# Two transformer blocks in float32 on one core: the low parts of 202 weight blocks made by an accumulating DMA

## The chip, the cores and the metric

The kernel runs on one core of a Trainium2 chip, as one program. Its metric is the device time of one execution in microseconds (us); the median of several executions counts.

## What is computed

Two stacks of two layers each, on 512 tokens of width 1024, all in float32. The first stack has a latent attention mixer (MLA) and a differential attention mixer, the second a convolution and pooling mixer ("even") and a mixer of forgetting attention and a long convolution ("odd"). Behind each mixer stand a residual and a layer norm, then a gated feed-forward layer, again with residual and norm:

```python
for i in range(DEPTH):
    mix = _mla_mixer(h, ...) if i % 2 == 0 else _diff_mixer(h, ...)
    h = _layernorm(ALPHA * h + mix, ln_mix_g[i], ln_mix_b[i])
    h = _layernorm(ALPHA * h + _swiglu(h, ffn_w_gu[i], ffn_w_down[i]), ln_ffn_g[i], ln_ffn_b[i])
for layer in range(DEPTH):
    mix = even_mixer(x, ...) if layer % 2 == 0 else odd_mixer(x, ...)
    x = layer_norm(ALPHA_2 * x + mix, ln_mix_g[layer], ln_mix_b[layer])
    x = layer_norm(ALPHA_2 * x + swiglu(x, ffn_w_in[layer], ffn_w_out[layer]), ...)

def _swiglu(x, w_gu, w_down):
    gate, up = jnp.split(x @ w_gu, 2, axis=-1)
    return (jax.nn.silu(gate) * up) @ w_down
```

Nearly all the work is matrix products with weights that are read once.

## The kernel before

**Split products.** TensorE works on a rounded type (F32R in the code). Each float32 operand is therefore kept as a high part, which is the operand rounded to F32R, and a low part, the operand minus the high part. `mm3` makes each product from three matmuls: high by high (L370), one high by low (L371) and the other (L372). Everything that a product reads needs its low part by the second or third matmul.

**Weights.** `weight_plan` lists 300 weight blocks of 128 partitions by up to 1024 columns (512 KB) in the order in which the stages use them. `Weights.load` (L162) fetches a block from HBM with a DMA on SyncE's queue (SP) into a tile `wraw`; there are two such tiles, taken in turn. `Weights.split` makes the high part `whi` on ScalarE (ACT, L169) and the low part `wlo` on VectorE (DVE) or, for a few, on GpSimd (POOL) (both L170); `whi` and `wlo` have five tiles each. So a `wraw` tile is free, and the load of the block after the next can start, when a block's low part has been made; and a `whi` tile is free when TensorE has used the block that stood in it. `Weights.ahead(n)`, called by hand in the order of the program, splits a few blocks ahead of use; `LOOK` is 2.

**Two forms of product.** 76 of the 300 entries ("win": most of the gate and up columns of the four feed-forward layers) are multiplied in a seven-product form, whose blocks are combined on VectorE first and come in four splits per entry through a `wraw` ring of their own. The other 224 are single splits: the mixers' projections (`mla_a`, `mla_b`, `uq_r`, `uq_n`, `ukv`, `df_q`, `df_k`, `df_v`, `ev_in`, `od_a`, `od_g`, `od_x`, `od_v`, `od_q`, `od_k`), their output projections (`mla_o`, `df_o`, `ev_o`, `od_o`), the first `gate` and `up` blocks of a feed-forward layer and all its `down` blocks.

**Stages.** MLA (to 201 us of the profiled span), feed-forward (to 554), differential attention (to 806), feed-forward (to 1158), even (to 1300), feed-forward (to 1651), odd (to 1891), feed-forward (to the end). One block is 24 matmuls of 512 columns, or as much work in other shapes.

**The seams.** A stage ends in `project_out`: the last products, then a layer norm per 128 tokens (sums on VectorE, squares on ScalarE, the root on GpSimd, gains and biases on VectorE), transposes on TensorE, high and low parts of the result. The first four products of the next stage are issued there too (`first`): over the first 256 tokens for blocks one to four, in between the last token tile's transposes, then over the other 256. In `project_out` the order on TensorE, VectorE and ScalarE is the order in which the code is written (`by_hand`); `W.ahead(2)`, `(3)`, `(4)` and `(5)` stand among it. Elsewhere a scheduler sets each engine's order. GpSimd also issues the DMAs of the norms' gains and biases (`lng`, `lnb`, L418) there, on a queue of its own.

Of the kernel before, what the change touches and what calls it, by code (L numbers as in the profile page):

```python
# [9 lines left out]
F32 = mybir.dt.float32  # L10
F32R = mybir.dt.float32r
BF16 = mybir.dt.bfloat16
AF = mybir.ActivationFunctionType
OP = mybir.AluOpType
# [38 lines left out]

ONPOOL = ("uq_n", "ukv", "df_o", "mla_o")
OTHERWISE = (11, 12, 15, 20, 23, 24, 25, 73, 79, 80, 81, 82, 83, 84, 85, 86, 88, 90, 91, 100, 102, 103)
NORM_ACT = (1, 3, 6, 7, 12, 13, 16, 24, 25, 26, 30)
ROPE_POOL = (1, 2, 3, 4, 5, 7, 9, 11)
DUP_ACT = (0, 2, 4, 6)
# [83 lines left out]
class Weights:  # L142
# [23 lines left out]
    def split(self, pool, raw, o, n, eng):  # L166
        tiles = [p.tile([P, UNIT], F32R, name="w" + k, tag="w" + k) for p, k in zip(pool, ("hi", "lo"))]
        hi, lo = [x[:, :n] for x in tiles]
        self.nc.scalar.activation(hi, raw[:, o:o + n], AF.Copy)  # L169
        eng.tensor_sub(lo, raw[:, o:o + n], hi.bitcast(F32))  # L170
        return tiles

    def steps(self):

        while self.loaded < min(len(self.plan), self.at + 2) and (
                self.loaded == self.at or self.plan[self.loaded][0] != "win" or self.sums is not None):
            self.load()
        name, raw, n = self.got[self.at]
        self.at += 1
        nc = self.nc  # L180
        if name != "win":
            on_pool = (name in ONPOOL) != (self.at - 1 in OTHERWISE)
            self.ready.append((name, *self.split((self.hi, self.lo), raw[0], 0, n, nc.gpsimd if on_pool else nc.vector)))
            return

        gate, up = raw
        H = UNIT // 2
        a11, a12, a21, a22 = gate[:, :H], gate[:, H:], up[:, :H], up[:, H:]
        pg = self.split((self.hi, self.lo), gate, 0, UNIT, nc.vector)
        yield  # L190
        pu = self.split((self.hi, self.lo), up, H, H, nc.vector)
        nc.vector.tensor_add(a22, a21, a22)
        nc.vector.tensor_sub(a21, a11, a21)
        yield
        su = self.split(self.sums, up, 0, UNIT, nc.vector)
        nc.vector.tensor_sub(a11, a22, a11)
        nc.vector.tensor_sub(a12, a12, a11)
        yield
        sg = self.split(self.sums, gate, 0, UNIT, nc.vector)

        def part(tiles, o):
            return [x[:, o:o + H].rearrange("p (k n) -> p k n", n=P) for x in tiles]

        self.ready.append((name, {
            1: part(pg, 0), 2: part(pg, H), 3: part(sg, H), 4: part(pu, 0), 5: part(su, H), 6: part(sg, 0), 7: part(su, 0)}, None))
# [107 lines left out]
def kernel(ctx: ExitStack, tc: tile.TileContext, a: dict, out: bass.AP):  # L313
# [393 lines left out]
    def ffn(xpool_cm, xT, key, i, ps, names):  # L707
# [3 lines left out]
        with pool("ffn") as fp:  # L711
# [3 lines left out]
            def hidden(j, g, u):  # L715
                nc.vector.tensor_mul(g, g, u)
                h = fp.tile([P, S], F32R, name="hh", tag="hh", bufs=HID)
                l = fp.tile([P, S], F32R, name="hl", tag="hl", bufs=HID)
                split(h, l, g)
                chunks[j] = (h, l)  # L720
# [112 lines left out]
    def mla(xT, close_x, open_x, names):  # L833
        with pool("mla_o") as op_:
            cmask = op_.tile([P, S], F32, name="cmask")
            with ExitStack() as st:
# [28 lines left out]
                def turn_c(j, h, l):  # L865
                    ps = pst()
                    for t in range(NT):
                        nc.tensor.transpose(ps[:, t * P:(t + 1) * P], cq[:, t, j * P:(j + 1) * P], ident)
                    split(h, l, ps, par("g_q", j) if j < 3 else par("g_kv", j - 3))
# [67 lines left out]
                def head(h):  # L937
                    p, i = divmod(h, 2)
                    if i == 0:
                        WP[p] = W.next("uq_n", 3, 256), W.next("ukv", 2, 512)  # L940
                    wq, wk = WP[p]
                    m = slice(i * P, (i + 1) * P)
                    got = []
                    for s, (w, k, x, sc) in enumerate((
                            (wq, 3, (cqh, cql), -MLA_SCALE),
                            (wk, 2, (ckh, ckl), None))):
                        ps = acc()
                        project_T(ps, w, x, k, m=m)
                        hi = ap_.tile([P, S], F32R, name="qh", tag=f"qh{s}", bufs=2)
                        lo = ap_.tile([P, S], F32R, name="ql", tag=f"ql{s}", bufs=2)  # L950
                        split(hi, lo, ps, sc)
                        got += [hi, lo]
                    Q[h] = got
# [39 lines left out]
                def rest(h, pt, qb, n, e, sums):  # L993
                    nc.vector.reciprocal(sums[:, 2:3], sums[:, 1:2])
                    if 4 * h + qb in NORM_ACT:
                        nc.scalar.activation(e[:, :n], e[:, :n], AF.Copy, scale=sums[:, 2:3])
# [905 lines left out]
```

## Time and profile before

| | us |
|---|---|
| three runs | 2255.45, 2256.09 (median), 2257.32 |
| the profiled execution | 2255.44 |
| its span, first to last instruction | 2253.7 |
| TensorE busy in the span | 2194.6 |
| VectorE busy | 1753.4 |
| ScalarE busy | 998.2 |
| GpSimd busy | 132.1 |

The mean granted TensorE clock over the span is 0.993. A busy TensorE counts pipelined matmuls whose ends overlap, so 97% is no statement on its peak; the idle rest, 59 us, is what all waits of TensorE together cost.

### The profile page before, as it was taken

To read this page: it belongs to the slowest core of one execution; us is meant where nothing else is said; L and a number is where in the kernel's file an instruction comes from. 1 tells how busy PE (TensorE), PEld (TensorE's weight loads), DVE (VectorE), ACT (ScalarE), POOL (GpSimd) and SP (SyncE) were. 2 spreads that over 40 slices of the span, in tenths; PEclk is the share of its full clock that TensorE was granted. 3 is DMA by queue.
4 is the path that set the end of the run, shared out by engine and by line. 5 is a ranking of instruction groups with operands and counts; after the bars stand their busy time and mean duration, and the time that the engine had idled before them with its cause. 6 is when DMAs were issued, how large, how long until landed. Compare 5 with 4: busy or idle time off the path is not lost. (4 is left out here: it accounts for less than half of the span.)

```text
span 2253.7 us, 35104 instructions
## 1 busy us (share of the span) xinstructions
PE 2194.6 (97%) x14076; PEld 1971.3 (87%) x14076; DVE 1753.4 (78%) x2871; ACT 998.2 (44%) x1669; POOL 132.1 (6%) x138
## 2 busy tenths in 40 slices
PE   8999999999999999999999999999999889999997
PEld 8888999998988789999988899999988767999996
DVE  5767988887666688888765588888679987988886
ACT  4654444333665554443333244433336655444331
POOL 2200000001321100000010000000010000000001
PEclk9999999999999999999999999999999899999999
DMA  5213332332321133333323233333232102233331
GB/s 174 64 48 103 94 113 94 113 94 75 111 79 63 47 108 107 104 94 113 94 98 95 75 131 107 104 100 108 90 99 93 57 19 103 94 113 94 113 94 56
DMA packets 59363, 210.48 MB, mean 93 GB/s; under 512 B 6624, under 2 KB 6880, under 8 KB 59200
## 3 DMA queue, kind: packets, MB, share of 16 engines
q1 hardware_dynamic: 56304, 198.97, 27.8%
q0 software_dynamic: 2320, 8.23, 1.1%
q8 instruction: 110, 1.80, 0.3%
q10 hardware_dynamic: 576, 1.05, 0.1%
q14 instruction: 53, 0.43, 0.1%
HBM read 206.12 MB, written 2.10 MB: 92 GB/s over the span
## 5 line engine op out<-in xcount | busy, mean ns | idle before, releaser
L169 ACT ACTIVATE whi<-wraw 128x1024 fp32r<-128x1024 f32 (+2 forms) x528 | 520.4, 988 | 838.8 <-PE acc L371 501.7
L170 DVE TENSOR_TENSOR wlo<-wraw,whi 128x1024 fp32r<-128x1024 f32 (+2 forms) x502 | 568.2, 1133 | 126.2 <-ACT whi L169 123.3
L371 PE MATMUL acc<-xl,whi 128*128 128x256 f32 (+1 forms) x1712 | 522.9, 305 | 3.5 <-DVE xl L480 3.5
L372 PE MATMUL acc<-xh,wlo 128*128 128x256 f32 (+1 forms) x1712 | 522.2, 305 | 2.6 <-DVE wlo L170 2.5
L370 PE MATMUL acc<-xh,whi 128*128 128x256 f32 (+1 forms) x1712 | 523.6, 306 | 0.4 <-DVE kl L1097 0.4
L371 PEld LDWEIGHTS acc<-xl,whi 128*128 128x128 f32 x1712 | 322.5, 188 | 29.2 <-DVE xl L480 4.7
L370 PEld LDWEIGHTS acc<-xh,whi 128*128 128x128 f32 x1712 | 322.4, 188 | 25.6 <-DVE kl L1097 0.5
L372 PE MATMUL acc<-xs,wlo 128*128 128x256 f32 x1216 | 341.3, 282 | 0.0
L371 PE MATMUL acc<-xql,whi 128*128 128x256 f32 x1216 | 341.0, 281 | 0.0
L372 PEld LDWEIGHTS acc<-xh,wlo 128*128 128x128 f32 x1712 | 322.6, 188 | 18.9 <-DVE wlo L170 3.8
L370 PE MATMUL acc<-xs,whi 128*128 128x256 f32 x1216 | 339.0, 280 | 0.0
L371 PEld LDWEIGHTS acc<-xql,whi 128*128 128x128 f32 x1216 | 228.5, 188 | 5.5
L370 PEld LDWEIGHTS acc<-xs,whi 128*128 128x128 f32 x1216 | 229.6, 189 | 3.5
L372 PEld LDWEIGHTS acc<-xs,wlo 128*128 128x128 f32 x1216 | 228.1, 188 | 0.3
L370 PE MATMUL tr<-whi,hh 128*128 128x512 f32 (+1 forms) x296 | 117.8, 398 | 0.0
L781 DVE TENSOR_TENSOR sums<-sums,acc 128x512 f32<-128x512 f32 x76 | 52.3, 688 | 83.9 <-PE acc L372 83.3
L371 PE MATMUL tr<-wlo,hh 128*128 128x512 f32 (+1 forms) x296 | 116.8, 395 | 0.0
L372 PE MATMUL tr<-whi,hl 128*128 128x512 f32 (+1 forms) x296 | 115.8, 391 | 0.0
L372 PE MATMUL ps<-whi,hl 128*128 128x512 f32 x288 | 113.7, 395 | 0.0
L370 PE MATMUL ps<-whi,hh 128*128 128x512 f32 x288 | 113.4, 394 | 0.0
L371 PE MATMUL ps<-wlo,hh 128*128 128x512 f32 x288 | 113.2, 393 | 0.0
L430 DVE SCALAR_TENSOR_TENSOR res<-res,acc 128x512 f32<-128x512 f32 x87 | 59.1, 683 | 58.1 <-PE acc L372 57.7
(364 smaller groups left out, 3959.5 us busy)
## 6 DMA issues: line engine op xcount, KB each, us to landing
wraw<-in_gu_dram SPq DMA_DIRECT2D x176, 512.0 KB, 3.5
wraw<-in_dn_dram SPq DMA_DIRECT2D x88, 512.0 KB, 3.4
wraw<-in_ev_in_dram SPq DMA_DIRECT2D x16, 512.0 KB, 3.5
wraw<-in_mla_o_dram SPq DMA_DIRECT2D x8, 512.0 KB, 3.5
wraw<-in_df_q_dram SPq DMA_DIRECT2D x8, 512.0 KB, 3.5
wraw<-in_df_k_dram SPq DMA_DIRECT2D x8, 512.0 KB, 3.5
wraw<-in_df_v_dram SPq DMA_DIRECT2D x8, 512.0 KB, 3.5
wraw<-in_df_o_dram SPq DMA_DIRECT2D x8, 512.0 KB, 3.4
```

Of the source, the lines that this page charges most:

```text
L169: self.nc.scalar.activation(hi, raw[:, o:o + n], AF.Copy)
L170: eng.tensor_sub(lo, raw[:, o:o + n], hi.bitcast(F32))
L370: nc.tensor.matmul(ps, ah, bh, start=first, stop=False)
L371: nc.tensor.matmul(ps, ah, bl, start=False, stop=False)
L372: nc.tensor.matmul(ps, al, bh, start=False, stop=last)
L430: nc.vector.scalar_tensor_tensor(y, y, ALPHA if first else 1.0, ps, op0=OP.mult, op1=OP.add, accum_out=SUMS[t][:, c:c + 1] if sums else None)
L781: nc.vector.tensor_add(g[:, 1:3], g[:, 1:3], v)
```

## The change

For blocks named in a new tuple, the low part no longer comes from one subtraction on VectorE or GpSimd. ScalarE writes the negated high part, rounded to F32R, into `wlo` (a second pass over `wraw`, with scale -1), and a DMA that GpSimd issues adds `wraw` to it in SBUF. The result is again the block minus its high part.

```diff
+BYDMA = ("od_x", "od_v", "od_q", "od_k", "od_o", "down", "df_q", "df_k", "df_v", "df_o", "ev_in", "ev_o", "mla_o", "gate", "up")
@@ split
         self.nc.scalar.activation(hi, raw[:, o:o + n], AF.Copy)
-        eng.tensor_sub(lo, raw[:, o:o + n], hi.bitcast(F32))
+        if eng is None:
+            self.nc.scalar.activation(lo, raw[:, o:o + n], AF.Copy, scale=-1.0)
+            self.nc.gpsimd.dma_start(lo.bitcast(F32), raw[:, o:o + n], accum_op=OP.add)
+        else:
+            eng.tensor_sub(lo, raw[:, o:o + n], hi.bitcast(F32))
@@ steps
-            self.ready.append((name, *self.split((self.hi, self.lo), raw[0], 0, n, nc.gpsimd if on_pool else nc.vector)))
+            self.ready.append((name, *self.split((self.hi, self.lo), raw[0], 0, n, None if name in BYDMA else nc.gpsimd if on_pool else nc.vector)))
```

By the plan 202 of the 300 blocks are named so: 181 were subtracted on VectorE and 21 on GpSimd. The 304 splits of the seven-product form and 22 blocks (`mla_a`, `mla_b`, `uq_r`, `uq_n`, `ukv`, `od_a`, `od_g`) stay as they were. Lines move by five: the high part is L170 in the new kernel, the negation L172, the DMA L173, the old subtraction L175.

The first place is ScalarE at the seam between the MLA mixer and its feed-forward layer, from the second block's high part on; `whi_2267`, `whi_2289` and `whi_2302` are the second, third and fourth block of the feed-forward layer (the old `up`, `gate`, `up`). Before:

```order
L169 ACTIVATE whi_2267<-wraw_2076 128x1024
L448 ACTIVATE junk_2281,lns_2243<-res3_81,lns_2243 128x1024
L169 ACTIVATE whi_2289<-wraw_2265 128x1024
L476 ACTIVATE xh_2055<-tr_2271 128x4x128
L476 ACTIVATE xh_2055<-tr_2276 128x4x128
L469 COPY xq_2060<-tr_2271 128x4x128
L169 ACTIVATE whi_2302<-wraw_2287 128x1024
```

And now, the same blocks with the numbers 2276, 2299 and 2313:

```order
L170 ACTIVATE whi_2276<-wraw_2084 128x1024
L172 ACTIVATE wlo_2277<-wraw_2084 128x1024
L453 ACTIVATE junk_2291,lns_2252<-res3_81,lns_2252 128x1024
L170 ACTIVATE whi_2299<-wraw_2274 128x1024
L172 ACTIVATE wlo_2300<-wraw_2274 128x1024
L481 ACTIVATE xh_2061<-tr_2281 128x4x128
L481 ACTIVATE xh_2061<-tr_2286 128x4x128
L474 COPY xq_2066<-tr_2281 128x4x128
L170 ACTIVATE whi_2313<-wraw_2297 128x1024
L172 ACTIVATE wlo_2314<-wraw_2297 128x1024
```

Each negation stands right behind its high part, and nothing else has moved.

The second place is GpSimd's queue at the same seam: `lnr` are the norms' roots, `lng` and `lnb` the loads of gains and biases. Before:

```order
L388 TENSOR_TENSOR lnr_2140<-lnv_2138,mhalf_93 128x1
L388 TENSOR_TENSOR lnr_2159<-lnv_2157,mhalf_93 128x1
L388 TENSOR_TENSOR lnr_2224<-lnv_2222,mhalf_93 128x1
L418 DMA lng_2548<-in_ln_ffn_g_dram 128x1024
L388 TENSOR_TENSOR lnr_2285<-lnv_2283,mhalf_93 128x1
L418 DMA lnb_2549<-in_ln_ffn_b_dram 128x1024
```

And now:

```order
L393 TENSOR_TENSOR lnr_2149<-lnv_2147,mhalf_93 128x1
L393 TENSOR_TENSOR lnr_2168<-lnv_2166,mhalf_93 128x1
L393 TENSOR_TENSOR lnr_2233<-lnv_2231,mhalf_93 128x1
L173 DMA wlo_2277<-wraw_2084 128x1024
L423 DMA lng_2562<-in_ln_ffn_g_dram 128x1024
L393 TENSOR_TENSOR lnr_2295<-lnv_2293,mhalf_93 128x1
L173 DMA wlo_2300<-wraw_2274 128x1024
L423 DMA lnb_2563<-in_ln_ffn_b_dram 128x1024
L173 DMA wlo_2314<-wraw_2297 128x1024
```

The DMAs of the second, third and fourth block stand between the roots and the loads; the fourth block's stands behind both loads.

The third place is TensorE in the MLA's output projection, where the last block of `mla_o` is first read (`whi_2072`, `wlo_2073` before; `whi_2079`, `wlo_2080` now). Before:

```order
L372 MATMUL acc_2082<-whi_1955,ol_2032 128x512
L370 MATMUL acc_2092<-whi_2072,oh_2014 128x512
L371 MATMUL acc_2092<-wlo_2073,oh_2014 128x512
L372 MATMUL acc_2092<-whi_2072,ol_2015 128x512
L370 MATMUL acc_2092<-whi_2072,oh_2031 128x512
L371 MATMUL acc_2092<-wlo_2073,oh_2031 128x512
```

And now:

```order
L377 MATMUL acc_2091<-whi_1960,ol_2038 128x512
L375 MATMUL acc_2101<-whi_2079,oh_2020 128x512
L375 MATMUL acc_2121<-whi_2072,oh_1679 128x512
L376 MATMUL acc_2121<-wlo_2073,oh_1679 128x512
L377 MATMUL acc_2121<-whi_2072,ol_1680 128x512
L375 MATMUL acc_2121<-whi_2072,oh_1799 128x512
L376 MATMUL acc_2121<-wlo_2073,oh_1799 128x512
L377 MATMUL acc_2121<-whi_2072,ol_1800 128x512
L375 MATMUL acc_2121<-whi_2079,oh_2020 128x512
L376 MATMUL acc_2101<-wlo_2080,oh_2020 128x512
```

Seven matmuls of another sum have moved between the first use of this block's high part and the first use of its low part.

## Rows read from the trace of the kernel before

**Rows 1.** The page, section 1: engine, busy us, share of the span, instructions.

```profile
PE 2194.6 (97%) x14076; PEld 1971.3 (87%) x14076; DVE 1753.4 (78%) x2871; ACT 998.2 (44%) x1669; POOL 132.1 (6%) x138
```

**Rows 2.** Waits of TensorE: engine, line, waited for; us in total, times, longest.

```profile
PE acc L371 <- DVE xl L480: 3.5, 6, 0.6
PE acc L372 <- DVE wlo L170: 2.5, 5, 0.8
```

**Rows 3.** Groups of instructions: shapes, count | busy us, mean ns | idle before, releasers.

```profile
L170 DVE TENSOR_TENSOR wlo<-wraw,whi 128x1024 fp32r<-128x1024 f32 (+2 forms) x502 | 568.2, 1133 | 126.2 <-ACT whi L169 123.3 <-PE acc L372 1.9
L169 ACT ACTIVATE whi<-wraw 128x1024 fp32r<-128x1024 f32 (+2 forms) x528 | 520.4, 988 | 838.8 <-PE acc L371 501.7 <-DMA wraw<-in_gu_dram 95.5 <-DVE wraw L193 58.7
```

**Rows 4.** DMA queues (packets, MB, share of 16 engines) and issues (KB, us to landing).

```profile
q1 hardware_dynamic: 56304, 198.97, 27.8%
...
wraw<-in_gu_dram SPq DMA_DIRECT2D x176, 512.0 KB, 3.5
...
lng<-in_ln_ffn_g_dram POOLq DMA_DIRECT2D x4, 512.0 KB, 4.8
lnb<-in_ln_ffn_b_dram POOLq DMA_DIRECT2D x4, 512.0 KB, 7.3
```

**Rows 5.** Timeline of ScalarE, first seam: start, duration, instruction, [idle before it].

```profile
180.16 1.06 ACT L169 ACTIVATE whi<-wraw 128x1024 fp32r<-128x1024 f32 x1 [0.34 <-PE acc L372]
...
199.31 1.08 ACT L169 ACTIVATE whi<-wraw 128x1024 fp32r<-128x1024 f32 x1
...
210.64 1.06 ACT L169 ACTIVATE whi<-wraw 128x1024 fp32r<-128x1024 f32 x1 [2.68 <-DMA wraw<-in_gu_dram]
```

**Rows 6.** Timeline of VectorE and of SyncE's queue, first seam.

```profile
203.83 1.22 DVE L170 TENSOR_TENSOR wlo<-wraw,whi 128x1024 fp32r<-128x1024 f32 x1
...
205.08 0.33 SPq L162 DMA_DIRECT2D wraw<-in_gu_dram  x1
```

**Rows 7.** Timeline of TensorE, first seam.

```profile
182.53 0.40 PE L370 MATMUL acc<-whi,oh 128*128 128x512 f32 x1
182.76 0.40 PE L371 MATMUL acc<-wlo,oh 128*128 128x512 f32 x1
...
213.01 0.39 PE L372 MATMUL acc<-xh,wlo 128*128 128x256 f32 x1 [0.68 <-DVE wlo L170]
```

**Rows 8.** Timeline of ScalarE and VectorE, seam into differential attention.

```profile
550.05 1.05 ACT L169 ACTIVATE whi<-wraw 128x1024 fp32r<-128x1024 f32 x1
...
557.02 1.22 DVE L170 TENSOR_TENSOR wlo<-wraw,whi 128x1024 fp32r<-128x1024 f32 x1
...
564.43 1.23 DVE L170 TENSOR_TENSOR wlo<-wraw,whi 128x1024 fp32r<-128x1024 f32 x1 [1.99 <-ACT whi L169]
```

**Rows 9.** Timeline of ScalarE, SyncE's queue and TensorE, end of the even mixer's output projection.

```profile
1271.46 1.06 ACT L169 ACTIVATE whi<-wraw 128x1024 fp32r<-128x1024 f32 x1 [16.34 <-issue]
...
1273.81 0.33 SPq L162 DMA_DIRECT2D wraw<-in_ev_o_dram  x1
...
1279.66 0.50 PE L371 MATMUL acc<-wlo,bh 128*128 128x512 f32 x1
```

**Rows 10.** Timeline of VectorE and TensorE, seam from the even mixer to its feed-forward layer.

```profile
1307.10 1.22 DVE L170 TENSOR_TENSOR wlo<-wraw,whi 128x1024 fp32r<-128x1024 f32 x1
...
1310.07 0.28 PE L372 MATMUL acc<-xh,wlo 128*128 128x256 f32 x1
```

**Rows 11.** Timeline of ScalarE and TensorE: a `down` block amid a feed-forward layer, and its last.

```profile
345.70 1.06 ACT L169 ACTIVATE whi<-wraw 128x1024 fp32r<-128x1024 f32 x1 [1.50 <-PE acc L371]
...
358.52 0.39 PE L371 MATMUL ps<-wlo,hh 128*128 128x512 f32 x1
...
526.49 1.06 ACT L169 ACTIVATE whi<-wraw 128x1024 fp32r<-128x1024 f32 x1 [8.15 <-PE acc L371]
...
533.18 0.63 PE L371 MATMUL acc<-wlo,hh 128*128 128x512 f32 x2
```

**Rows 12.** Stretches of the odd mixer: length, busy us (instructions) per engine, clock, DMA.

```profile
1680.00:1820.00 140.00, 129.22 (x684) 105.65 (x682) 136.87 (x271) 92.08 (x194) 0.00 (x0) 0.95 0.23 72
1760.00:1840.00 80.00, 65.77 (x315) 50.25 (x314) 76.51 (x166) 53.44 (x140) 0.00 (x0) 0.89 0.09 27
```

## The prediction, made before the changed kernel ran

> **What bounds the kernel now.** I read the page's busy times first: TensorE is busy 97% of the span [rows 1]. That figure is no peak, but it says that all its waits together cost 59 us, so no relief of another engine can bring more than a part of that. Then TensorE's waits: for low parts of weights it waited 2.5 us in five waits [rows 2]. The change therefore takes work off VectorE, 181 subtractions of about 1.2 us and some 220 us in all [rows 3], that TensorE hardly waits for. What decides is the other side: whether the new way of making a low part is late for TensorE. So I followed single blocks through the timelines: when the high part ends, when TensorE first asks for the low part, and when the raw tile comes free for the next load. I call the time from the end of the high part to the first use of the low part the cover of a block.
>
> Amid a feed-forward layer the cover is large: a high part ends at 346.76 and its low part is read at 358.52, so 11.8 us [rows 11]. At a seam between two stages it is almost nothing: the fourth block's high part ends at 211.70, and TensorE was already waiting when the low part came and its matmul started at 213.01 [rows 5, 7]. The reason is the two raw tiles. SyncE issues that load at 205.08, the moment the subtraction that frees the tile ends (203.83 and 1.22 make 205.05) [rows 6], and ScalarE waits for the load until 210.64 [rows 5]. The whole chain of subtraction, load, high part, subtraction lies on TensorE's path there.
>
> **The price of one low part.** Before: one subtraction of 1.2 us [rows 6]. After: a pass of ScalarE of 1.06 us [rows 5], and then a DMA, of which the trace has none that accumulates. Call its time from issue to landing L and bound it by rows. The nearest are GpSimd's own DMAs of the same 512 KB: 4.8 us for the gains and 7.3 us for the biases, the second of a pair at a busy seam; SyncE's plain loads land in 3.5 us [rows 4]. Such a DMA also has to fetch its target. The load queue took 27.8% of 16 engines for 2253.7 us, over 56304 packets: 178 ns for one [rows 4]. A block is 128 rows of 4 KB, eight packets for each of 16 engines, 1.4 us; a second stream of reads adds as much. I take L = 4.8 + 1.4 = 6.2 us, as an estimate, nearest to the gains' row. The ends that I keep are 4.8 (the second stream costs nothing) and 9 (7.3 and a second stream, or a unit that adds slowly). A low part is then ready 1.06 + 6.2 = 7.3 us after its high part, where it was 1.2 us.
>
> The Trainium skill would make it cheaper: "DMA: Bandwidth & Descriptors", in the section on the anatomy of a DMA on the GpSimd path, gives 2.0 us and the bytes over 436 GB/s, which is an estimate of 3.2 us for this block. The trace does not agree for plain DMAs of this size on that queue, which took 4.8 and 7.3 us, so I keep it as a rival only.
>
> **The seams.** Six seams have DMA-made blocks as second to fourth. At the first, the second block's high part ends at 200.39 [rows 5]; the order puts its negation directly behind, to 201.45, and GpSimd's queue has nothing waiting ahead of it. It lands at 207.65, which frees the raw tile 2.6 us later than 205.05. The load takes as long as before (205.08 to 210.64, 5.6 us), so the fourth block's high part runs from 213.24 to 214.30, its negation to 215.36, and it lands at 221.56: 8.6 us later than 213.01. On GpSimd's queue it stands behind both norm loads, which are out by then. The stalls of the second and third block are smaller, and lie within these 8.6. Three seams are of this kind: behind MLA, behind differential attention, behind odd. Into differential attention and into even the old subtraction was itself late, 557.02 after a high part that ended at 551.10 [rows 8]: negated by 552.16 and landed by 558.36, the block frees its tile no later than 558.24, and only the second half of the chain counts, 1.06 + 6.2 - 1.2 = 6.1. From even to feed-forward the fourth low part was ready at 1308.32 for a use at 1310.07 [rows 10], so 8.6 less 1.8, 6.8. Into the odd mixer the first four blocks stay with VectorE. Together 3 x 8.6 + 2 x 6.1 + 6.8 = **44.8 us**.
>
> **Output projections.** The last block of `mla_o` gets its slot at 180.16, and its low part is read at 182.76 [rows 5, 7]. The order now negates first, to 181.22; it lands at 187.4. Seven moved matmuls at 0.23 us each [rows 7] put the question off to 184.4: 3.0 us. In the even mixer the sixth `ev_o` block starts at 1271.46 and used to free its tile at 1273.81 [rows 9]; negated first, it lands at 1278.7. Then load 3.5, two passes 2.1, DMA 6.2: the last block is there at 1290.5 for a use at 1279.66 [rows 9], 10.8 us. Together **13.8 us**. For `df_o`, whose cover is larger, I charge nothing and keep 3 in the range.
>
> **The raw ring.** Where blocks follow each other at TensorE's full pace, one takes 24 matmuls of 0.23 us, 5.6 us [rows 7]. Two raw tiles now give one block per (3.5 + 1.06 + 1.06 + 6.2 + 0.6 of small waits) / 2 = 6.2 us. Over the 28 blocks of `ev_in`, `od_x`, `od_q` and `od_k` that is up to 17 us; they are prepared up to five slots ahead, which has to be eaten first, so I charge a third, **6 us**. At L = 9 the period is 7.6 and the whole 56 us show.
>
> **Feed-forward layers.** The cover of 11.8 us hides 7.3 for the `down` blocks; what hides it is the seven-product work between them, and if L passes 10.7 each of some 80 blocks stalls. Only the last block of a layer has less: its high part ends at 527.55 and its low part is read at 533.4, the second of the pair [rows 11], 5.9 us, short by 1.4 in three layers: **4.2 us**.
>
> **What comes back.** In the odd mixer VectorE is busy 136.9 of 140 us, and TensorE is idle 14.2 of the 80 us from 1760 on, at a lowered clock of 0.89 [rows 12]. Some 20 subtractions leave VectorE there. I credit half of the idle time, **7 us**. At the seams two subtractions leave VectorE's row of norm work; ScalarE gets as many passes. I credit **4 us**. GpSimd's 202 issues and ScalarE's 202 passes (44% busy [rows 1]) cost nothing where no norm or softmax waits for them; I found no place where a DMA stands ahead of a root and waits longer than the root.
>
> **Sum.** 44.8 + 13.8 + 6 + 4.2 - 7 - 4 = 57.8 us. The profiled execution took 2255.44 us, of which the span is 2253.7; with 57.8 it is 2313.2. The median of the runs is 0.65 above the profiled one: **2314 us**.
>
> **How it moves with L.** L counts twice in the chain at four seams and once at two, twice in `ev_o`, once in the other places, and weakly in the ring: some 20 us for each us of L. At 4.8 the sum is 30 and the time 2286. At 9 it is 114, and 50 for the whole ring: 2420.
>
> **Rivals.** (1) The adding costs no more than a copy, L = 4.8 or little above: 2286. For it: the row of the gains. Against it: a target has to be read. (2) The DMA is slow, L = 9 or more: raw ring and seams both bind, 2420. For it: the biases' 7.3 us at exactly these seams, where norm loads, weight loads and the new DMAs would meet. (3) L = 3.2, the page's formula: the losses shrink by 60 and meet the relief, 2254 to 2258, no change. The rows of 4.8 and 7.3 speak against it. (4) Faster, by one mechanism: in the odd mixer all of TensorE's idle 14.2 us come back [rows 12], because VectorE is what attention waits for there. It decides only if L is below about 3; the time would be near 2247. That the change does not do what it says I rule out: the order has 202 such DMAs.
>
> **How the numbers follow.** Forecast (L between 5 and 8.5, 2288 to 2390) 0.62; copy price 0.14; slow 0.17; no change 0.03; faster 0.04. About 0.2%, 4.5 us, is what a measurement of this kernel can tell from no change. The range reaches from 2280 to 2420, leaving out some 0.2: most of the last two cases, the lower part of the copy price, the upper part of the slow one. Faster 0.04, same 0.03, slower 0.93.
>
> **What would show it.** In the new profile: the accumulating DMAs' landing time, near 6; waits of TensorE for a low part or its DMA of 6 to 9 us at each of six seams and of about 11 before the end of `ev_o`; nearly none amid feed-forward layers and at the seam into odd; less idle TensorE after 1760 in the odd mixer. It is wrong if these DMAs land in under 4 us, or in over 10, or if TensorE's new waits are for something else, such as a norm held up behind a DMA on GpSimd.

## The result, and the profile of the changed kernel

The changed kernel takes 2374.05 us (median of 2370.62, 2372.75, 2375.34 and 2377.4) against 2256.04 for the kernel before: a ratio of 1.0522, with a 95% interval of 1.0504 to 1.054. That is 118 us slower where 58 were forecast. The direction was right and the time lies inside the range, but the sum was half of what came. The profiled execution took 2377.4 us, its span 2375.6.

The page's busy times, against [rows 1]:

```profile
PE 2232.4 (94%) x14076; PEld 1999.0 (84%) x14076; DVE 1550.4 (65%) x2690; ACT 1173.7 (49%) x1871; POOL 250.2 (11%) x319
```

VectorE lost 203 us of work, as the change intended. TensorE has the same 14076 matmuls and is still busy 38 us longer, at a mean clock of 0.974 (0.993 before), and its idle rest grew from 59 to 143 us. Its waits, against [rows 2] (engine, line, waited for: us in total, times, longest):

```profile
PE acc L377 <- DMA wlo<-wraw: 46.1, 15, 6.8
PE acc L376 <- DMA wlo<-wraw: 8.3, 4, 5.1
PE ps L375 <- ACT plh L382: 7.6, 3, 4.0
PE ps L1594 <- ACT kk L1430: 5.6, 1, 5.6
```

Nineteen waits for an accumulating DMA make 54 us; before, five waits for a low part made 2.5. The longest of the other new waits are for ScalarE, of which more below. The DMA queues and issues, against [rows 4]:

```profile
q1 hardware_dynamic: 56304, 198.97, 25.2%
q0 software_dynamic: 31408, 113.13, 24.3%
...
wlo<-wraw POOLq DMA_DIRECT2D x198, 512.0 KB, 4.7
wraw<-in_gu_dram SPq DMA_DIRECT2D x176, 512.0 KB, 4.4
...
lng<-in_ln_ffn_g_dram POOLq DMA_DIRECT2D x4, 512.0 KB, 5.4
lnb<-in_ln_ffn_b_dram POOLq DMA_DIRECT2D x4, 512.0 KB, 9.6
```

The median accumulating DMA lands 4.7 us after its issue, faster than the 6.2 us of the forecast. By the forecast's own table 4.7 us should have meant about 2285. So one size was too high and others far too low.

**Where the time went.** I cut both traces at the same matmul of TensorE, counted from the start, so that a stretch holds the same work in each, and took the difference in length. "Seams" are the six stretches of 51 to 85 us around those boundaries at which the changed kernel waits; each includes the end of the stage ahead. The forecast's terms are put in the stretches in which they fall (seams 44.8, last `down` 4.2, `mla_o` 3.0 and norms -4 make the 48.0; the 6 of the ring stand in halves).

| difference from before, us | forecast | changed | e4 | e3 | e2 | e6 |
|---|---|---|---|---|---|---|
| MLA mixer | 0 | 1.9 | 4.3 | 1.7 | 1.8 | 1.6 |
| six seams | 48.0 | 72.0 | 5.6 | 36.7 | 69.2 | 9.2 |
| differential attention | 0 | 7.7 | 5.4 | 2.4 | 5.9 | 4.3 |
| even, input blocks | 3 | 11.3 | 0 | 0 | 0 | 4.2 |
| even, end of `ev_o` | 10.8 | 11.6 | 0.9 | 8.3 | 11.8 | 12.5 |
| odd, first blocks | 3 | 26.3 | 3.7 | 7.1 | 1.9 | 29.4 |
| odd, rest | -7 | -10.8 | 3.2 | -10.4 | -11.5 | -10.7 |
| inside the feed-forward layers | 0 | 0.5 | 0.3 | 0.3 | 6.5 | 0.9 |
| sum | 57.8 | 120.5 | 23.4 | 46.1 | 85.6 | 51.4 |

The sum for the changed kernel, 120.5, stands against 121.9 between the two spans. The columns on the right are experiments, told below. Inside the feed-forward layers, where most of the 88 `down` blocks are, nothing was lost, as forecast. The two large misses are the seams (+24) and the first blocks of the even and odd mixers (37.6 where 6 were charged).

### The profile page after: what moved, and what is told of

It reads as the page before. It is cut to its first block, busy times and chain, and to the rows that moved or that the text cites. A ratio compares the mean times of both kernels' runs of the same rounds, so it can differ in the third digit from the quotient of the medians.

```text
span 2375.6 us, 35585 instructions
## 1 busy us (share of the span) xinstructions
PE 2232.4 (94%) x14076; PEld 1999.0 (84%) x14076; DVE 1550.4 (65%) x2690; ACT 1173.7 (49%) x1871; POOL 250.2 (11%) x319
## 3 DMA queue, kind: packets, MB, share of 16 engines
q0 software_dynamic: 31408, 113.13, 24.3%
## 4 chain that ended last, share of the span: by engine, by line
PE 67%; DMA 15%; issue 6%; DVE 5%; ACT 5%; POOL 1%; SPq 0%; POOLq 0%; DVEq 0%; ACTq 0%
PE acc L377 16%; PE acc L375 16%; PE acc L376 16%; DMA wlo<-wraw 8%; PE ps L377 3%; PE ps L376 3%; PE ps L375 3%; PE tr L375 3%; PE tr L376 3%; PE tr L377 3%; DMA wraw<-in_ev_in_dram 1%; ACT wlo L172 1%; ACT whi L170 1%; DMA wraw<-in_ev_o_dram 1%; DMA wraw<-in_gu_dram 1%
## 5 line engine op out<-in xcount | busy, mean ns | idle before, releaser
L170 ACT ACTIVATE whi<-wraw 128x1024 fp32r<-128x1024 f32 (+2 forms) x528 | 519.4, 986 | 874.9 <-PE acc L376 352.4
L377 PE MATMUL acc<-xh,wlo 128*128 128x256 f32 (+1 forms) x1712 | 535.3, 313 | 46.4 <-DMA wlo<-wraw 46.1
L376 PE MATMUL acc<-xl,whi 128*128 128x256 f32 (+1 forms) x1712 | 533.7, 312 | 3.3 <-DVE xl L485 3.3
L375 PE MATMUL acc<-xh,whi 128*128 128x256 f32 (+1 forms) x1712 | 535.6, 313 | 0.4 <-DVE kl L1102 0.4
L175 DVE TENSOR_TENSOR wlo<-wraw,whi 128x1024 fp32r<-128x1024 f32 (+3 forms) x321 | 347.9, 1085 | 146.5 <-ACT whi L170 145.9
L377 PEld LDWEIGHTS acc<-xh,wlo 128*128 128x128 f32 x1712 | 333.5, 195 | 65.9 <-DMA wlo<-wraw 49.7
L173 POOL DMA_DIRECT2D wlo<-wraw x202 | 174.4, 863 | 1808.5 <-ACT wlo L172 1317.4
L376 PEld LDWEIGHTS acc<-xl,whi 128*128 128x128 f32 x1712 | 333.6, 195 | 29.6 <-DVE xl L485 4.5
L375 PEld LDWEIGHTS acc<-xh,whi 128*128 128x128 f32 x1712 | 333.9, 195 | 25.5 <-DVE kl L1102 0.5
L172 ACT ACTIVATE wlo<-wraw 128x1024 fp32r<-128x1024 f32 (+1 forms) x202 | 210.2, 1041 | 28.4 <-PE acc L376 25.6
```

The source lines that it names most:

```text
L172: self.nc.scalar.activation(lo, raw[:, o:o + n], AF.Copy, scale=-1.0)
L173: self.nc.gpsimd.dma_start(lo.bitcast(F32), raw[:, o:o + n], accum_op=OP.add)
L375: nc.tensor.matmul(ps, ah, bh, start=first, stop=False)
L376: nc.tensor.matmul(ps, ah, bl, start=False, stop=False)
L377: nc.tensor.matmul(ps, al, bh, start=False, stop=last)
```

## A seam, read closely

The first seam in the changed kernel, on the same engines as [rows 5] to [rows 7] (start, duration, instruction, idle before it and what ended it); first GpSimd's queue:

```profile
207.34 0.89 POOL L173 DMA_DIRECT2D wlo<-wraw  x1 [3.21 <-PE tr L403]
209.56 0.56 POOL L423 DMA_DIRECT2D lng<-in_ln_ffn_g_dram  x1 [1.33 <-DVE lnv L391]
...
210.66 0.91 POOL L173 DMA_DIRECT2D wlo<-wraw  x1
212.33 0.56 POOL L423 DMA_DIRECT2D lnb<-in_ln_ffn_b_dram  x1 [0.77 <-DVE res L465]
221.05 0.86 POOL L173 DMA_DIRECT2D wlo<-wraw  x1 [8.16 <-ACT wlo L172]
```

ScalarE's fourth high part, and TensorE's three waits:

```profile
218.76 1.06 ACT L170 ACTIVATE whi<-wraw 128x1024 fp32r<-128x1024 f32 x1 [7.21 <-DMA wraw<-in_gu_dram]
```

```profile
211.87 0.39 PE L377 MATMUL acc<-xh,wlo 128*128 128x256 f32 x1 [1.13 <-DMA wlo<-wraw]
218.56 0.38 PE L377 MATMUL acc<-xh,wlo 128*128 128x256 f32 x1 [2.70 <-DMA wlo<-wraw]
227.63 0.58 PE L377 MATMUL acc<-xh,wlo 128*128 128x256 f32 x1 [4.48 <-DMA wlo<-wraw]
```

The chain is the forecast one: the second block's DMA is issued at 207.34 and lands as TensorE goes on at 211.87; the freed raw tile is loaded; that load lands at 218.76; the fourth block's DMA goes out at 221.05 and TensorE has it at 227.63. From the end of the second block's high part (206.10; 200.39 before) to this use it is 21.5 us, 12.6 before: 8.9 us more, where 8.6 was forecast. But the parts differ. The second block's DMA took 4.5 us, not 6.2, the third's 7.8 and the fourth's 6.5, and the load 6.8 instead of 5.6. DMA issues alone show it: first the stretch of the seam, 205 to 232, then 300 to 520, amid the feed-forward layer (count, KB, median us to landing).

```profile
wraw<-in_gu_dram SPq DMA_DIRECT2D x5, 512.0 KB, 6.9
wlo<-wraw POOLq DMA_DIRECT2D x4, 512.0 KB, 7.0
```

```profile
wraw<-in_gu_dram SPq DMA_DIRECT2D x28, 512.0 KB, 4.3
wlo<-wraw POOLq DMA_DIRECT2D x14, 512.0 KB, 4.6
```

A single L for all places was the wrong tool: it is 4.6 where there is cover, and 7.0 just where there is none.

## The experiments

Each is a change to the changed kernel, unless it says otherwise. Ratios are to the kernel before, timed beside it, with a 95% interval.

**e1 and e13: TensorE kept at work during the waits.** Behind the waits the granted clock falls to its lower level, and the 38 us of extra busy time looked like a second price of each wait.

```diff
             for i, name in enumerate(names):
                 w.append(W.next(name, KD, P, look=0))
+                for _ in range(FILL[i] if name in BYDMA else 0):      # FILL = (0, 10, 22, 36)
+                    nc.tensor.matmul(first[i][:, 0:256], w[i][0][:, 0], xT[0][:, 0, 0:256], start=True, stop=True)
                 project_T(first[i], w[i], xT, KD, 0, 256)
```

> The changed kernel, and TensorE repeats the first matmul of the second, third and fourth block at a seam 10, 22 and 36 times (256 columns, about 0.117 us each, 8 us a seam) before it asks for the low part; these sums are overwritten, so the result is unchanged. Theory: of the 118 us lost, about 83 are waits of TensorE and about 35 a granted clock that falls to its lower level behind these waits (0.93 to 0.96 over the 60 to 90 us of a seam). With the waits filled by work the clock stays at 1.00 there and each of six seams gives back 3 to 5 us: 2346 to 2356. Rival: the clock falls for another reason than idle time (the DMA traffic of the seam, the norm): the clock is as low as now and the time 2372 to 2385.

Measured: 2377.03 us, ratio 1.0549 (1.0531 to 1.0567): no gain. The time is the rival's, but not its reason, for the mean clock rose from 0.974 to 0.984. The six seams together were 69.4 us longer than before, not 72.0; behind the even mixer the repeated work outlasted the waits (13.7 us longer, 7.2 in the changed kernel), so this run did not decide. The second form fits the number to each wait:

> As the run with repeated matmuls, but their number is fitted to the waits: of the second to fourth block 10, 21, 50 behind MLA, 0, 32, 33 into differential attention, 10, 22, 49 behind it, 0, 18, 30 into even, 0, 50, 0 behind even, 10, 28, 47 behind odd (256 columns, 0.117 us each; before the low part is asked for; overwritten). Theory: the low parts land when the DMA chain lets them, at either clock, so the filled time is no gain; only the slow matmuls behind a seam's last wait are: in the changed kernel TensorE falls behind by 1.5 to 4.5 us more from the last wait to the end of a seam's stretch, 15 us over six seams. 2355 to 2366. Rival (the clock costs more than that, since slow matmuls also delay the chain): under 2350. Rival (the clock has no share): 2370 to 2378.

Measured: 2379.7 us, ratio 1.0552 (1.0533 to 1.0571): no gain again, and the range I gave was missed. Stretches behind the first seam (length, TensorE busy, granted clock, DMA share, GB/s), the changed kernel and then e13:

```profile
211.00:219.00 8.00, 4.42 (x35) 1.00 0.95 243
219.00:228.00 9.00, 4.52 (x24) 0.73 0.79 254
228.00:236.00 8.00, 8.00 (x49) 0.67 0.57 133
```

```profile
211.00:219.00 8.00, 7.92 (x66) 1.00 0.96 247
219.00:228.00 9.00, 8.63 (x73) 1.00 0.81 255
228.00:236.00 8.00, 8.00 (x68) 1.00 0.66 138
```

The clock of 0.73 and 0.67 is a mix of its two levels, 2.4 and 1.2 GHz; in e13 it was held at the upper one, and still TensorE gets the fourth low part no sooner, at 227.87 (227.63 above):

```profile
227.87 0.39 PE L383 MATMUL acc<-xh,wlo 128*128 128x256 f32 x1 [0.37 <-DMA wlo<-wraw]
```

The chain that brings it does not run on TensorE. Only the slow matmuls behind the last wait are lost. Over the six seams the stretches are 64.1 us longer than before instead of 72.0, so the clock's share is some 8 us there by one profiled execution of each, and even these did not reach the total (other stretches, the odd mixer's first blocks and the feed-forward layers above all, came out longer in this run; why is open). TensorE is busy 22 of the 38 us more at the seams; some 14 of these, then, are matmuls that run slowly in time that would have been idle. For the other 16 no run shows it.

**e3: the same DMA without the adding.**

```diff
-            self.nc.gpsimd.dma_start(lo.bitcast(F32), raw[:, o:o + n], accum_op=OP.add)
+            self.nc.gpsimd.dma_start(lo.bitcast(F32), raw[:, o:o + n])
```

> The changed kernel with a plain DMA copy from the raw tile into the low tile, nothing added (so the low parts, and the result, are wrong). It prices the adding. Theory: the DMA's time is mostly issue, descriptors and completion, and the adding itself a small part: landing 3.9 to 4.6 us where the accumulating one took 4.7, the time 2350 to 2374. Rival: the adding is what is slow: landing under 3.7, the time under 2345.

Measured: 2303.08 us, ratio 1.0217 (1.0202 to 1.0233). The rival was right. The queue and the issues in this run:

```profile
q0 software_dynamic: 31152, 113.13, 12.5%
...
wlo<-wraw POOLq DMA_DIRECT2D x198, 512.0 KB, 2.9
```

The same 113.13 MB take 12.5% of the DMA engines' time in a span of 2301.2 us as a copy, 288 us, and 24.3% of 2375.6 us with the adding, 577 us: twice as much. The median landing goes from 2.9 to 4.7 us. These 1.8 us per DMA, with the weight loads that land sooner beside the copy (3.7 instead of 4.4 us for the largest group), are worth 71 us of the kernel: 39 for each us of L, where I had worked out 20. The Trainium skill ("DMA: Bandwidth & Descriptors", anatomy of one DMA on the GpSimd path) gives an estimate of 3.2 us for such a block; for the plain copy (2.9 us) the trace agrees nearly, for the accumulating one (4.7 us) it does not. "Collectives: The Full Stack", in the Trainium skill, on the bandwidth ceiling, says of ReduceScatter that it is slower than a copying collective because the add needs two source reads; twice the engine time here fits that, but no run here shows which reads take it.

**e4: ScalarE's second pass alone**, with the block added to the negated high part by the engine that subtracted before.

```diff
+            eng.tensor_add(lo, raw[:, o:o + n], lo.bitcast(F32))
-            self.nc.gpsimd.dma_start(lo.bitcast(F32), raw[:, o:o + n], accum_op=OP.add)
```

> The changed kernel, but the negated high part gets the block added by VectorE (or GpSimd, for the 21 blocks that it had before), not by a DMA. It prices ScalarE's second pass alone. Theory: 1.06 us more in the chain, once or twice per seam, 1 to 2 us at six seams and little elsewhere: 2258 to 2272. Rival (ScalarE's passes hold up norms and attention work in its queue): over 2285.

Measured: 2280.23 us, ratio 1.0113 (1.0098 to 1.0128), 25 us, between the two theories. Only 5.6 us of it lie at the seams. The mixers pay most, 4.3 in MLA, 5.4 in differential attention, 6.9 in the odd one: there ScalarE's queue also holds the high parts of attention, and a pass more can stand ahead of one. Two of TensorE's waits in this run, the second for such a high part, and then that wait before:

```profile
PE acc L378 <- DVE wlo L174: 7.5, 5, 1.7
...
PE acc L376 <- ACT vh L383: 5.2, 1, 5.2
```

```profile
PE acc L370 <- ACT vh L377: 2.6, 1, 2.6
```

That is 2.6 us more in the odd mixer, and the waits for low parts are 5.0 us longer than before (2.5 in [rows 2]). No row here accounts for the rest of the 25 us.

**e2: the raw tile freed early.** The accumulating DMA reads the block from HBM again.

```diff
-            self.nc.gpsimd.dma_start(lo.bitcast(F32), raw[:, o:o + n], accum_op=OP.add)
+            self.nc.gpsimd.dma_start(lo, eng.bitcast(F32R), accum_op=OP.add)     # eng: the block in HBM
```

> The changed kernel, but the accumulating DMA reads the block from HBM again instead of from the raw tile, so that the raw tile is free after ScalarE's two passes. Theory (raw tiles held through the DMA): the next load no longer waits for the DMA. The rings of the even mixer's input and of the odd mixer's first blocks (11.3 and 21.4 us longer than before) and the end of the even mixer's output projection (11.6) give back nearly all, 35 to 44 us, and each of six seams one of the two DMA times in its chain, 4 to 6 us and the clock behind it: 2285 to 2310. Rival (the lateness of each low part by itself, about 6 us behind its high part, is what costs): 2360 to 2375. Rival (the doubled traffic slows the loads): no better than 2365, with loads landing later than 4.4 us.

Measured: 2341.32 us, ratio 1.0394 (1.0371 to 1.0417). The forecast time was missed, and the rival of slower loads held in part: these DMAs land in 6.8 to 8.4 us instead of 4.7, and the largest group of weight loads in 5.3 instead of 4.4. So the seams gained next to nothing (69.2), the end of `ev_o` nothing, and the feed-forward layers lost 6.5. The even mixer's input blocks and the odd mixer's first blocks gave back nearly everything, 11.3 to 0 and 26.3 to 1.9, although each low part was later. What costs there is the raw tile, not the low part.

**e6: the old subtraction for the first six blocks of the six stages.**

```diff
-None if name in BYDMA else nc.gpsimd ...
+None if name in BYDMA and self.at - 1 not in SEAMS else nc.gpsimd ...
+SEAMS = {i + k for i in (26, 73, 105, 152, 176, 253) for k in range(6)}
```

> The changed kernel, but the first six blocks of the six stages at whose start TensorE waited for a DMA keep the old subtraction. Theory: the six seams, 66 of the 118 us with their share of the lowered clock, come back except for ScalarE's part: 2300 to 2320; what is left is the end of the even mixer's output projection, the rings of the even and odd mixers, differential attention, less the odd mixer's gain. Rival (a seam is late because the DMAs of the stage before it are, or because of the norm loads): 2335 or more.

Measured: 2310.19 us, ratio 1.0238 (1.0224 to 1.0252), as expected. 36 blocks carried 63 of the 72 us at the seams. Six of them each are differential attention's and the even mixer's first blocks, and these stretches fell too (7.7 to 4.3, 11.3 to 4.2); the end of `ev_o` and the odd mixer are within about 3 us of the changed kernel. Of the 9.2 us that are left at the seams, 5.0 lie at the one into differential attention, where e5 shows a cause.

**e5: only the 88 `down` blocks** (`BYDMA = ("down",)`).

> The change for the 88 down blocks of the feed-forward layers alone. Theory: their cover (low part landed 3 to 6 us ahead of its use amid a layer in the changed kernel) hides pass and DMA; the last blocks of a layer may stall by 1 us or so: 2254 to 2262, no change. Rival (the DMAs' traffic and the second pass slow the stages whatever the cover): over 2266.

Measured: 2266.28 us, ratio 1.0046 (1.0032 to 1.006): 10 us, not the nothing that I expected. The time is at the edge of the rival's range, but its reason did not hold: inside the layers the stretches are within 0.5 us of before. 5.4 us of the profiled execution lie at the end of the first layer, and 2.4 behind the last matmul of the program, where I know no cause. ScalarE at the end of the first layer, in e5 and then before:

```profile
536.79 1.06 ACT L170 ACTIVATE whi<-wraw 128x1024 fp32r<-128x1024 f32 x1 [6.38 <-DMA wraw<-in_df_q_dram]
537.76 0.61 ACT L382 ACTIVATE hh<-sums 128x512 fp32r<-128x512 f32 x1
```

```profile
532.18 0.63 ACT L377 ACTIVATE hh<-sums 128x512 fp32r<-128x512 f32 x1 [3.07 <-DVE sums L716]
```

The last hidden unit's high part (`hh`) stands behind the high part of the next stage's first block on ScalarE, and that one waits 6.38 us for a load which waits for a raw tile that a DMA holds. TensorE waits for no DMA-made low part in this run.

**e11 and e12: without the norm's loads at the seams**, in the changed kernel and in the one before.

```diff
     def ln_params(key, i, queue=nc.gpsimd):
+        if GB:
+            return GB[0]
...
+        GB.append((g, b))
```

> The changed kernel with the gains and biases loaded once and used for every norm (so seven pairs of loads of 512 KB are left out, and the result is wrong). It asks why the DMAs at a seam took 6.5 to 9 us where those amid a layer took 4.4. Theory (they share queue and engines with the norm's loads): 5 us or less at the seams, two such DMAs in a chain, 2340 to 2358. Rival (they only meet the weight loads, which stay): 2366 to 2375.

> The kernel before with the same loads left out, for comparison: its seams wait 0.7 us for a low part at two places and the fourth block's load took 5.6 us there. 2252 to 2256; what the run beside it gains over this comes from the new DMAs.

Measured: 2358.73 us (ratio 1.0459, 1.0445 to 1.0473), just above the theory's range, and 2250.75 (0.998, 0.9971 to 0.9989), just below the one that I gave. The loads cost the changed kernel 15.3 us and the old one 5.5, so 10 us come from the new DMAs meeting them; by the seams' stretches (72.0 to 50.7, and 0 to -4.4) it is 17. The accumulating DMAs of the first seam landed in 4.9 us there (7.0 with the loads).

**e7, e8, e9, e10: the odd mixer alone.** Here the change gained 10.8 us, and I asked what of it can be had. All four are the kernel before with the new way for a few blocks: the twelve latest (e7); the same twelve subtracted by GpSimd instead (e8); all of `od_x`, `od_v`, `od_q`, `od_k` and `od_o`, reading HBM as in e2 (e9) or the raw tile (e10).

> The kernel before, with the new way for twelve blocks alone: the last four od_q and od_k and the eight od_o, made while VectorE is the busy engine of the odd mixer. In the changed kernel this stretch was 10.8 us shorter than before, and these blocks were ready 8 us and more ahead of their use. Theory (the gain there is VectorE's relief and doesn't need the rest): 6 to 11 us faster than before, 2244 to 2250. Rival (the stretch was shorter only because the stretch before it was late and had done attention's work ahead): 2253 to 2260.

> The kernel before, with the same twelve blocks subtracted by GpSimd in place of VectorE, without DMA and without ScalarE's second pass. Theory (what helps is that VectorE is relieved, by whichever means): the same as the run with the DMA within 3 us, 2244 to 2252. Rival (GpSimd's subtraction of 2.4 us or more slows VectorE beside it): 2255 or more.

> The change for od_x, od_v, od_q, od_k and od_o alone (26 blocks), and their accumulating DMA reads the block from HBM again, so that the raw tile is free after ScalarE's two passes. In the run with all blocks made so, the odd mixer's stretches were 1.0, 0.9 and -11.5 us from before. Theory (VectorE's relief over the whole odd mixer gives the gain, the raw tiles took it back): 2245 to 2250, faster than before. Rival (the gain needed a late mixer, or goes with what the twelve late blocks gave, 2 us): 2253 to 2257.

> The same 26 blocks, with the DMA reading the raw tile as in the changed kernel. Theory (two raw tiles, each held for load, two passes and DMA, give a block each 6.8 us where TensorE uses one in 5.6): the first stretches of the odd mixer lose 25 to 30 us and the rest gains 10: 2271 to 2279. Rival (the lateness comes from the stages ahead): under 2262.

| | us | ratio (95%) | odd, first blocks | odd, rest |
|---|---|---|---|---|
| e7 | 2253.76 | 0.9993 (0.9984 to 1.0002) | 0.6 | -4.3 |
| e8 | 2263.40 | 1.0038 (1.0025 to 1.005) | 2.5 | 5.6 |
| e9 | 2249.82 | 0.9967 (0.9955 to 0.998) | 0.8 | -11.5 |
| e10 | 2275.76 | 1.009 (1.0074 to 1.0105) | 25.9 | -10.6 |

e7 came out in its rival's range: its stretch is 4.3 us shorter, but the total is not clear of the noise. e9 and e10 came as their theories said. e9 is faster than both kernels, by 6.5 us than the one before. It and e10 differ only in what the DMA reads. The odd mixer's first blocks, before, in e9 and in e10 (length, TensorE, its weight loads, VectorE, ScalarE, GpSimd, clock, DMA share, GB/s):

```profile
1705.00:1749.60 44.60, 44.15 (x251) 37.51 (x250) 43.77 (x77) 32.21 (x61) 0.00 (x0) 1.00 0.24 77
```

```profile
1707.00:1752.40 45.40, 44.23 (x251) 37.52 (x250) 44.58 (x83) 38.25 (x67) 6.04 (x7) 1.00 0.76 178
```

```profile
1709.60:1777.60 68.00, 52.20 (x252) 42.17 (x251) 47.52 (x89) 44.09 (x73) 7.91 (x9) 0.85 0.65 150
```

With the raw tile held, the same matmuls take 68 us instead of 45. What TensorE waits for there in the changed kernel is, but for 2.3 us, not even a low part: 5.6 us for `kk`, 4.7 for a tile of VectorE's, 2.8 for `kb`, 1.5 for `e`. ScalarE at the longest of these waits, and then TensorE:

```profile
1839.20 1.06 ACT L170 ACTIVATE whi<-wraw 128x1024 fp32r<-128x1024 f32 x1 [3.44 <-DMA wraw<-in_od_qk_dram]
1840.16 1.04 ACT L172 ACTIVATE wlo<-wraw 128x1024 fp32r<-128x1024 f32 x1
1841.23 1.28 ACT L1430 ACTIVATE kk<-kb 64x512 fp32r<-64x512 f32 x2
```

```profile
1841.91 0.47 PE L1594 MATMUL ps<-kk,qq 128*128 128x128 f32 x1 [5.57 <-ACT kk L1430]
```

In these rows ScalarE takes its work in order: the high part of a block that isn't loaded yet holds up `kk`, and `kk` holds up TensorE. SyncE issued the loads of the odd mixer's first blocks at 1789.00, 1795.04, 1802.07, 1808.88 and 1815.13, one in 6.5 us; TensorE needs one in 5.6. In the even mixer's input blocks, too, TensorE waits for ScalarE: all its 7.6 us of idle time there are the three waits for `plh` shown at the top.

For e8 the rival held, and rows tell how; VectorE's `cv` group in the odd mixer's stretch, before and in e8 (count | busy us, mean ns | idle before):

```profile
L1370 DVE SCALAR_TENSOR_TENSOR cv<-gl,sm,cv 128x512 f32<-128x512 f32 x101 | 71.6, 742 | 0.4
```

```profile
L1376 DVE SCALAR_TENSOR_TENSOR cv<-gl,sm,cv 128x512 f32<-128x512 f32 x101 | 88.5, 909 | 0.3
```

Twelve subtractions on GpSimd relieve VectorE of 15 us and make 101 of its other instructions 17 us longer in sum. The mean hides how: nine of these instructions, each beside a subtraction on GpSimd, took 2.1 to 2.9 us, and none of the others more than 0.76. One of them, GpSimd first:

```profile
1739.28 2.39 POOL L176 TENSOR_TENSOR wlo<-wraw,whi 128x1024 fp32r<-128x1024 f32 x1 [5.40 <-ACT whi L171]
```

```profile
1739.66 2.56 DVE L1376 SCALAR_TENSOR_TENSOR cv<-gl,sm,cv 128x512 f32<-128x512 f32 x1
```

In e7, where the same twelve blocks go by DMA, the mean of the 101 stays at 745 ns.

## The prediction, point by point

The direction and most of the places were right; the sum failed on sizes. The stretches lost 63 us more than forecast. Of these the raw ring makes 32 (charged with 6 us, measured 37.6) and the seams 24 (48, measured 72). Most of the rest lies in differential attention, put at nothing: 7.7 us, and 5.4 with ScalarE's passes alone (e4).

- **What bounds the kernel: right.** What VectorE was spared hardly counted, and waits of TensorE, most of them for low parts, did; the seams, the end of `ev_o`, the odd mixer's gain and the covered `down` blocks came where they were put.
- **L = 6.2: wrong as one number.** 4.7 as a median, 4.6 under cover, 7.0 at the first seam. The two rows that bounded it come close to these, which is partly luck, since they are plain loads: the gains' 4.8, and the biases' 7.3, taken at a busy seam. I took the gains' row and 1.4 us for every place, where the seam's row should have priced the seams. The copy alone lands in 2.9 us, not 4.8, and the adding, which I charged with 1.4 us, costs 1.8 (e3).
- **Seams: mechanism right, mis-sized.** 48 with the layer ends was forecast, 72 measured. The chain behind MLA was 8.9 for 8.6 us, which is luck in part: the first DMA was faster than forecast, the later ones and the load slower. The rest are, for the most part, DMAs and loads that meet the norm's loads (10 to 17 us, e11 with e12) and slow matmuls behind the last wait (about 8 us, e13). Into differential attention, 6.1 was forecast and 13.3 came. This stretch holds the layer's end, too, which alone made it 5.4 us longer in e5. Seen from the second block's high part, the first raw tile was free no later, as said, but its load took 6.7 us (issued at 578.3) and the two DMAs behind 8.1 and 6.4; the load's own delay was not in my sum.
- **The raw ring: the step that failed most.** The blocks "are prepared up to five slots ahead, which has to be eaten first, so I charge a third", 6 of 17 us. Measured: 37.6 us at the two places, and e9 against e10 shows for the odd mixer that it is the ring: 0.8 or 25.9 us by what the DMA reads (e2 shows it for the even one). The period was 6.5 us, not far from 6.2, but the lead that I counted on saved nothing that a run shows, and a late load does not only delay its block: it blocks ScalarE, and with it high parts of activations (`kk`, `plh`) that I had not in the sum. The clock of 0.84 to 0.85 in the odd mixer's first blocks came on top.
- **ScalarE's passes "cost nothing": wrong.** e4 prices them at 25 us, of which 17 in the three attention mixers. I had looked for norms and softmax behind a DMA on GpSimd, not for high parts behind a pass on ScalarE. One wait shows that (`vh`, 2.6 us more); for the rest it is not shown.
- **`ev_o` and `mla_o`: right in size, in part by luck.** 11.6 for 10.8, but 3.2 of the 11.6 are slower matmuls, which I had not charged. The wait at the last `mla_o` block is 1.50 us, half of the 3.0 forecast; with what follows it TensorE is 3.3 us further behind by the seam's second block.
- **Last `down`: wrong in cause, the size met by luck.** Not 1.4 us in each of three layers, but 5.4 at the end of one and under 0.6 at the others (e5), and no wait for a `down` low part; instead ScalarE's queue.
- **Relief: right for the odd mixer** (-10.8 for -7; e9 shows that it is VectorE's relief, since it stays when the stretch ahead is not late, and in e4, where VectorE keeps its work, the stretch is 3.2 us longer). For the norms, 4 us, no run shows it.
- **"Some 20 us for each us of L": wrong**, it is 39 by the medians of e3. By the table the difference lies at the seams (35 us), in the ring's two places (30), in differential attention (5) and at the end of `ev_o` (3). I had let the ring move weakly with L.

## What to carry over

Price a wait with the durations of the place where it happens, taken from rows of that stretch, and not with a median over the kernel: what shares the queue at a seam is what makes it a seam. Where a producer and a consumer run through a ring of two buffers, compare the two periods and charge the whole difference, unless the trace shows a lead (here 17 us, which is still short of 37.6); and look at what else stands in the queue of the engine that waits for the buffer. A step that relieves a busy engine is worth taking only at the place where that engine is waited for, and only if it holds no buffer on the way: 26 blocks gave 6.5 us with the DMA reading HBM (e9) and cost 19.5 with the raw tile held (e10); 202 cost 118.

## What the runs showed of the hardware

- The accumulating DMAs within SBUF held the DMA engines twice as long as copies of the same bytes (24.3% of 2375.6 us and 12.5% of 2301.2 us, each with 8 MB of other DMAs on that queue), and landed in 4.7 instead of 2.9 us.
- With the source read from HBM they were slower still, 7.2 us for the `down` blocks (e2).
- The granted clock was 0.67 to 0.73 in the stretches behind waits of 2.7 and 4.5 us; holding it at 1.00 with repeated matmuls gave back 8 of 72 us at the seams and nothing of the total, since the waits ended when DMAs landed (e13).
- Nine VectorE instructions of 742 ns took 2.1 to 2.9 us beside a GpSimd subtraction of some 2.4 us (e8); the mean of 909 ns over 101 hides it.
